# Rounded w_down factors made among the factors of q and k, weight loads two blocks ahead of rounding, and weight sums in other places

## The chip, the cores and the metric

One core of one Trainium2 chip runs the whole program. The metric is the device time of one execution in microseconds; the time before is the median of three runs, 1922.76 us (1920.47 to 1925.07). The core has five engines that run their own instruction streams in order and wait for one another by semaphores: PE multiplies matrices, ACT and DVE and POOL work elementwise, and SP issues most of the transfers (POOL issues the rest). Sixteen DMA engines move the data for all of them.

## The reference, cut to what matters

The kernel computes one layer of an encoder over 512 tokens of width 2048: a mixing part (attention of 8 heads beside a pooling part of 4 groups) and a feed-forward part (FFN) with a gate and a causal convolution.

```
h = rms_norm(x, pre_mix_g)
z = h @ w_in                      # q | k | v of 8 heads, and u
a = chunked_attention(q, k, v, rel_bias)
p = multiscale_pool(u, pool_w, pool_scale)
x = x + rms_norm(concatenate([a, p]) @ w_o, post_mix_g)
h = rms_norm(x, pre_ffn_g)
up = causal_dwconv(h @ w_up, conv_w, conv_b)
y = (gelu(up[:F]) * up[F:]) @ w_down
x = x + rms_norm(y, post_ffn_g)
```

Everything is float32. F is 5632.

## The kernel before

**Precision.** A float32 matrix goes to PE as two rounded parts: `split` (L138, L139) rounds it to a high part on ACT, and subtracts that from the source on DVE for the low part. `mm3` (L160, L162, L163) multiplies high by high, low by high and high by low. `mm2` (L168, L174) does a product that is 512 wide with the high part and 256 wide with the low one.

**Fast products.** q and k of heads 1 to 7, w_o and the FFN are multiplied in seven products of half-size blocks in place of eight. Some of the blocks are sums of weight blocks. For q and k they are made on DVE in the tiles where the weights were loaded. For w_o and w_down 1 MB sums are made in DRAM by transfers alone: `sums_in_dram` yields one copy, or one add onto a copy, at a time, and `more_sums(n)` takes the next n. There are 48 (32 for w_o, then 16 for w_down). While `paced` is set, they stand in POOL's queue behind a marker that waits for work that the program issued before; later, copies go through SP.

**Stages** and where they stand in the trace: q and k of head 0 (0 to 22 us); the first half of v (to 66, `v_steps(0)`); q and k of heads 1 to 7, the pairs (to 206); the second half of v beside the attention of heads 0 to 2 (to 282); u0 to u7 beside the other heads and the pooling (to 427); w_o (to some 590); then the FFN, whose first w_up products stand in a stage of their own (w10), and whose w_down products end the program.

**Weights.** Ordinary weights go through `Weights`: a list of blocks in the order of use, each a load of 512 KB on SP into a raw tile and a `split` into a hi and a lo tile of the ring `w4`; `prefetch` issues load and split together, three blocks ahead of PE.

**Pairs.** `Pairs` does the same for q and k. One pair k (one head) has seven products i; the products of neighbouring pairs are interleaved: (k+1,1), (k,6), (k+1,2), (k,7), (k+1,5), (k,4), (k+1,3). `load` (L467) loads four blocks per pair, named wx, ww, wz and wy; `make` splits the next factor (wfh, wfl) into the ring `w4`, which has four pairs of tiles, and then makes the next sum in place. `qk_product` and `qk_keep` multiply and take the products out of PSUM: products 1, 6, 7 and 4 of a pair share bank "a", which ACT empties (za, zm, zm, z) between them. At the end of a pair q and k go to DRAM (zqk, L596); the attention reads them back by head (zq, L673), multiplies by the norm's factor on DVE (L678) and splits them (qkh, qkl).

**Ready factors.** Three blocks of w_down, in six parts of 512 KB (`ready_parts`), are needed twice in rounded form. Each part (rw) is loaded, split, and its hi and lo halves are stored to DRAM (`ready_w`) during the u stage. Before, this is one more entry in the list of `Weights`: it stands behind the blocks of u0 to u5, in tiles of the ring `raw`, and `keep_ready` stores the halves (L284).

**Order.** PE's order is written out by hand in the program text. The other engines' orders, SP's queue among them, come from a scheduler that takes the instructions of the text as they become possible.

Of the kernel before, what the change touches and what calls it, by code (L numbers as in the profile page):

```python
# [15 lines left out]
P = 128  # L16
# [29 lines left out]
def f32(ap):  # L46
    return ap.bitcast(F32)
# [7 lines left out]
class Weights:  # L55


    def __init__(self, specs, load, ahead):
        self.specs, self.load, self.ahead, self.tiles, self.used = specs, load, ahead, [], 0
        self.limit = len(specs)  # L60

    def prefetch(self, n=None):
        self.prefetch_to(self.used + (self.ahead if n is None else n))
# [1 line left out]
    def prefetch_to(self, upto):  # L65
        upto = min(self.limit, upto)
        while len(self.tiles) < upto:
            self.tiles.append(self.load(*self.specs[len(self.tiles)]))

    def get(self, name, ahead=None):  # L70
        assert self.specs[self.used][0] == name, (self.specs[self.used][0], name)
# [8 lines left out]
def encoder_layer(ctx: ExitStack, tc: tile.TileContext, x, xT, vecs, rel, post_mix, post_ffn,  # L80
# [65 lines left out]
    def load_w(name, src, a, b):  # L146
        n = a * b
        raw = raw4(name + "r")
        if name[:2] == "rw":
            hi, lo = (big.tile([P, 1024], F32R, tag="raw", bufs=5, name=name + p) for p in "hl")  # L150
        else:
            hi, lo = w4(name + "h"), w4(name + "l")
        flat_ = len(src.shape) == 2
        load_w.last = nc.sync.dma_start(
            raw[:, :n] if flat_ else raw[:, :n].rearrange("p (a b) -> p a b", a=a), src).ins
        split(hi[:, :n], lo[:, :n], raw[:, :n])
        return tuple(v[:, :n].rearrange("p (a b) -> p a b", a=a) for v in (hi, lo))

# [102 lines left out]
    READY_AT = {0: (), 1: ()}  # L261
    ready_parts = [(at, j) for at in READY for j in range(2)]
    READY_OF = {0: (), 1: ready_parts}
    READY_U = {j: j for j in range(6)}

    def ready_spec(at, j):
        cc, i = at
        return (f"rw{cc}{i}_{j}", first_block(cc, i - 1, 0)[:, 2 * j:2 * j + 2, :], 2, 512)

    def v_and_ready_specs(g):  # L270
        specs = []
        for n, spec in enumerate(v_specs(g)):
            specs.append(spec)
            if n in READY_AT[g]:
                specs.append(ready_spec(*READY_OF[g][READY_AT[g].index(n)]))
        return specs

    def keep_ready(g, n):
        at = READY_U if g else {m: k for k, m in enumerate(READY_AT[0])}
        if n not in at:  # L280
            return
        (cc, i), j = READY_OF[g][at[n]]
        for dest, v in zip(ready_w[cc, i], weights.get(f"rw{cc}{i}_{j}")):
            nc.sync.dma_start(dest[:, 2 * j:2 * j + 2, :], f32(v))  # L284

    specs = v_and_ready_specs(0)
    FIRST_PART = len(specs)
    specs += v_and_ready_specs(1)
    for g in range(4):
        specs += u_specs(2 * g)  # L290
        if g:
            specs += pm_spec(g - 1)
        if 2 * g in READY_U:
            specs.append(ready_spec(*READY_OF[1][READY_U[2 * g]]))
        specs += u_specs(2 * g + 1)
        if 2 * g + 1 in READY_U:
            specs.append(ready_spec(*READY_OF[1][READY_U[2 * g + 1]]))
    for i in WO:
        for cc in range(2):
            specs += wo_specs(i, cc)  # L300
# [4 lines left out]
            specs += [(f"w{p}{u}_{i}", w_up[u, p, :, i // 2, :, i % 2 * 512:(i % 2 + 1) * 512].rearrange(  # L305
                "m p c -> p m c"), 2, 512) for i in range(4)]

    weights = Weights(specs, load_w, 3)
    weights.limit = FIRST_PART


# [38 lines left out]
                yield  # L350

    sums_step = sums_in_dram()


    RR = const.tile([P, 2, S], F32, name="RR")
# [41 lines left out]
    def v_steps(i, ps):  # L397
        for n, c in enumerate(VORDER[i]):
            w = weights.get(f"v{i}_{c}", 2 if (i, n) == (1, 0) else None)
            if not i:  # L400
                pairs.prefetch(3 - FIRST_PART + weights.used)
            for j in range(2):
                kb = 2 * c + j
                for t in range(NT):
                    mm3(ps[t], g_tokens(hT, kb, t), part(w, j), n == j == 0, n == 7 and j == 1)
                if j and not i:
                    keep_ready(i, n)
                    pairs.prefetch(3 - FIRST_PART + weights.used)
                yield

# [41 lines left out]
    class Pairs:  # L452
# [3 lines left out]
        def __init__(self):  # L456
            n = self.n = HEADS - 1
            place_of = {1: 0, 2: 2, 5: 4, 3: 6, 6: 8, 7: 10, 4: 12}
            begin = [(0, 1), (0, 2), (0, 5), (1, 1), (0, 3)]
            order = [(k, i) for _, k, i in sorted((7 * k + at, k, i) for k in range(n) for i, at in place_of.items())]  # L460
            self.order = begin + [at for at in order if at not in begin]
            self.order.insert(-2, (None, 0))
            self.raw, self.made, self.loaded, self.used = {}, [], 0, 0

        def load(self, k, i):
            def raw(what, tile_, m, kh):
                load_w.last = nc.sync.dma_start(tile_, w_qk[k + 1, m, kh]).ins  # L467
                self.raw[k, what] = tile_

            if i == 1:  # L470
                raw("x", raw4("wx") if not k else p0.tile([P, 1024], F32, tag="wx", bufs=3, name="wx"), 0, 0)
                raw("w", raw4("ww"), 1, 0)
            elif i == 2:
                raw("z", raw4("wz"), 0, 1)
            elif i == 5:
                raw("y", raw4("wy") if k else p0.tile([P, 1024], F32, tag="wx", bufs=3, name="wy"), 1, 1)

        def make(self, k, i):
            if k is None:
                weights.prefetch_to(FIRST_PART + 1)  # L480
                self.made.append(None)
                return
            x, w, y, z = (self.raw.get((k, what)) for what in "xwyz")
            hi, lo = w4("wfh"), w4("wfl")
            split(hi, lo, {3: y, 7: y, 2: z}.get(i, x))
            if i == 1:
                nc.vector.tensor_add(x, x, w)
            elif i == 5:
                nc.vector.tensor_add(x, x, y)
            elif i == 6:  # L490
                nc.vector.tensor_add(x, x, z)
            elif i == 3:
                nc.vector.tensor_add(y, y, w)
            self.made.append(tuple(v.rearrange("p (a b) -> p a b", a=8) for v in (hi, lo)))
# [11 lines left out]
                weights.prefetch_to(FIRST_PART + 1 + over)  # L506

        def get(self):
            self.used += 1
# [30 lines left out]
    def more_sums(n):  # L540
        for _ in range(n):
            next(sums_step, None)

    more_sums.paced = True

    BANK = {1: "a", 6: "a", 7: "a", 4: "a", 5: "g", 3: "g", 2: "d"}
    FIRST = 1, 5, 2
# [58 lines left out]
    for k, i in [at for at in pairs.order if at[0] is not None]:  # L606
        if k == pairs.n - 1 and i in (7, 4):
            if not steps:
                psv = [bank(f"v1_{t}") for t in range(NT)]
                steps = v_steps(1, psv)  # L610
                pairs.used += 1
# [19 lines left out]
    with tc.tile_pool(name="p1", bufs=2, reuse_waits="tile") as p1:  # L631
# [188 lines left out]
        for j in range(8):  # L820
# [62 lines left out]
    with tc.tile_pool(name="p2", bufs=1, reuse_waits="tile") as p2:  # L883
# [156 lines left out]
        for q in range(5):  # L1040
# [6 lines left out]
            if q:  # L1047
                gate_part(q - 1, 2)
                weights.prefetch(q)
        keep_x(2, turn_back.last)  # L1050
        for q in range(4):
# [696 lines left out]
```

## Time and profile before

| | before |
|---|---|
| median of 3 runs | 1922.76 us |
| lowest, highest | 1920.47, 1925.07 us |
| the profiled execution's own time | 1923.98 us |
| its span | 1922.2 us |
| its mean granted clock | 0.987 |
| PE busy | 1873.5 us, 97% |
| DVE, ACT, POOL busy | 80%, 56%, 16% |
| moved by DMA | 426.01 MB, 222 GB/s |

The durations below come from the profiled execution, whose span is the time from its first to its last instruction. A row of waits names the waiting instruction, the one that released it, and the total, the number and the longest of the waits in us. In a row of the chain of waits stand start, length and what ran; a DMA in it is the time from issue to landing. In a row of DMA issues stand the count, the size of one, and the median from issue to landing. q1 is SP's queue, q0 POOL's.

### The profile page before, as it was taken

What the parts mean: (1) busy time and instruction counts of PE and PEld (TensorE: products, weight loads), DVE (VectorE), ACT (ScalarE), POOL (GpSimd) and SP (SyncE); (2) the same over time, 40 slices, a digit from 0 to 9 for tenths busy, and PEclk for the clock granted to TensorE, in tenths of its full rate; (3) what the DMA queues carried; (4) which work ended last, traced back from release to release, by engine and by line L of the source; (5) the groups of instructions that cost most, each with busy time, mean ns of one, the idle gap of its engine ahead of it and who ended that gap; (6) DMA issues with size and microseconds to landing.
All of it is one profiled execution on the core that took longest, in us unless ns stands there. A gap on an engine that the chain in (4) does not pass through costs nothing.

```text
span 1922.2 us, 25415 instructions
## 1 busy us (share of the span) xinstructions
PE 1873.5 (97%) x9598; PEld 1593.1 (83%) x9598; DVE 1540.0 (80%) x1800; ACT 1082.9 (56%) x1376; POOL 301.5 (16%) x398
## 2 busy tenths in 40 slices
PE   9999989798999999999999999999999999999998
PEld 7888777676888888888888888888888888888886
DVE  6987667656778888888787888888887799898875
ACT  8655445334646566656566656656565665565553
POOL 3211110110000022222212121222211001101101
PEclk9999989898999999999999999999999999999999
DMA  7389988899787488888888888898988977876785
GB/s 257 123 264 287 328 204 307 216 309 273 263 250 283 140 212 202 200 196 199 208 200 200 204 199 205 200 199 195 208 188 273 349 228 176 197 197 171 172 237 143
DMA packets 139770, 426.01 MB, mean 222 GB/s; under 512 B 11968, under 2 KB 15424, under 8 KB 133952
## 3 DMA queue, kind: packets, MB, share of 16 engines
q0 software_dynamic: 54864, 173.56, 44.9%
q1 hardware_dynamic: 84784, 250.84, 37.4%
q8 instruction: 75, 1.23, 0.2%
q14 instruction: 47, 0.39, 0.1%
HBM read 370.35 MB, written 104.33 MB: 247 GB/s over the span
## 4 chain that ended last, share of the span: by engine, by line
PE 88%; DMA 6%; DVE 3%; ACT 2%; issue 1%; SPq 0%; DVEq 0%; POOL 0%; POOLq 0%; ACTq 0%
PE qa L168 18%; PE qa L174 10%; PE qg L168 9%; PE qg L174 5%; PE qd L168 5%; PE pa L160 4%; PE pa L162 4%; PE pa L163 4%; PE qd L174 2%; DMA rw_0r<-in_w_down 2%; PE m L163 2%; PE m L162 2%; PE m L160 2%; PE pg L160 2%; PE pg L162 2%; PE pg L163 2%
## 5 line engine op out<-in xcount | busy, mean ns | idle before, releaser
L138 ACT ACTIVATE wfh<-wx 128x1024 fp32r<-128x1024 f32 x192 | 203.5, 1060 | 153.8 <-PE qg L168 58.8
L168 PE MATMUL qa<-gT,wfh 128*128 128x512 f32 x1152 | 289.1, 393 | 0.0
L139 DVE TENSOR_TENSOR wfl<-wx,wfh 128x1024 fp32r<-128x1024 f32 x192 | 234.8, 1223 | 61.2 <-ACT wfh L138 45.5
L168 PEld LDWEIGHTS qa<-gT,wfh 128*128 128x128 f32 x1152 | 207.0, 188 | 37.5
L1365 POOL DMA_DIRECT2D wx<-in_w_up x122 | 104.6, 857 | 506.2 <-DVE wfl L139 478.0
L138 ACT ACTIVATE wfh<-wy 128x1024 fp32r<-128x1024 f32 x96 | 101.9, 1061 | 118.7 <-PE qg L168 62.0
L168 PE MATMUL qg<-h,wfh 128*128 128x512 f32 x656 | 165.7, 394 | 0.0
L174 PE MATMUL qa<-gT,wfl 128*128 128x256 f32 x1152 | 160.6, 282 | 0.0
L174 PEld LDWEIGHTS qa<-gT,wfl 128*128 128x128 f32 x1152 | 151.0, 190 | 4.4
L168 PEld LDWEIGHTS qg<-h,wfh 128*128 128x128 f32 x656 | 122.9, 188 | 28.0
L139 DVE TENSOR_TENSOR bl<-b,bh 128x2048 fp32r<-128x2048 f32 x56 | 127.4, 2288 | 22.5 <-ACT bh L138 11.7
L138 ACT ACTIVATE bh<-b 128x2048 fp32r<-128x2048 f32 x56 | 105.8, 1912 | 48.5 <-DVE b L1123 20.5
L139 DVE TENSOR_TENSOR wfl<-wy,wfh 128x1024 fp32r<-128x1024 f32 x96 | 117.2, 1221 | 14.2 <-ACT wfh L138 7.8
L160 PE MATMUL pa<-bh,ah 128*128 128x512 f32 x320 | 126.1, 394 | 0.0
L162 PE MATMUL pa<-bl,ah 128*128 128x512 f32 x320 | 125.8, 393 | 0.0
L163 PE MATMUL pa<-bh,al 128*128 128x512 f32 x320 | 125.5, 392 | 0.0
L139 DVE TENSOR_TENSOR wfl<-wz,wfh 128x1024 fp32r<-128x1024 f32 x48 | 58.8, 1224 | 55.2 <-PE qa L168 55.2
L168 PE MATMUL qd<-gT,wfh 128*128 128x512 f32 x384 | 95.7, 391 | 0.0
L174 PEld LDWEIGHTS qg<-h,wfl 128*128 128x128 f32 x656 | 89.4, 188 | 7.5
L174 PE MATMUL qg<-h,wfl 128*128 128x256 f32 x656 | 91.6, 282 | 0.0
L168 PEld LDWEIGHTS qd<-gT,wfh 128*128 128x128 f32 x384 | 72.0, 188 | 16.2
L168 PE MATMUL qa<-h,wfh 128*128 128x512 f32 x328 | 83.2, 395 | 0.0
(552 smaller groups left out, 4390.0 us busy)
## 6 DMA issues: line engine op xcount, KB each, us to landing
wx<-in_w_up POOLq DMA_DIRECT2D x122, 512.0 KB, 5.9
b<-in_w_down SPq DMA_DIRECT2D x32, 1024.0 KB, 6.8
wt<-in_w_o POOLq DMA_DIRECT2D x24, 1024.0 KB, 12.6
wx<-in_w_up SPq DMA_DIRECT2D x43, 512.0 KB, 5.5
wz<-in_w_up SPq DMA_DIRECT2D x41, 512.0 KB, 5.6
wy<-in_w_up SPq DMA_DIRECT2D x41, 512.0 KB, 4.6
wy<-in_w_up POOLq DMA_DIRECT2D x41, 512.0 KB, 6.2
sum<-part POOLq DMA_DIRECT2D x38, 512.0 KB, 6.1
```

What stands on the lines that cost most here:

```text
L138: rounded = nc.scalar.activation(hi, src, AF.Copy)
L139: rest = nc.vector.tensor_sub(lo, src, f32(hi))
L160: nc.tensor.matmul(ps, l[0], r[0], start=first, stop=False, skip_group_check=onto)
L162: nc.tensor.matmul(low, l[0], r[1], start=False, stop=False, skip_group_check=onto)
L163: nc.tensor.matmul(ps, l[1], r[0], start=False, stop=last, skip_group_check=onto)
L168: nc.tensor.matmul(ps, w[0][:, kb], pairs[kb][0], start=fresh and not kb, stop=last, skip_group_check=not fresh)
L174: nc.tensor.matmul(ps[:, sl], w[1][:, kb], pair[:, sl], start=False, stop=last, skip_group_check=not fresh)
L1365: nc.gpsimd.dma_start(self.raw[k, what], self.block(k, m, kh), accum_op=ALU.add)
```

## The change

`Weights` is now given a loader and a maker: a block is loaded `raws` = 2 blocks before it is split. `ready_spec`, `v_and_ready_specs` and `keep_ready` are gone; the six rw parts are entries (None, m) in the list of `Pairs`, each behind (m, 7). Their raw tile is one of its own (tag rw), hi and lo are a pair of `w4`, and the two stores are issued at the start of the next `make`. The sums are taken elsewhere: four more in the V stage (n = 4, 7, 10, 13), one fewer in the first head, six fewer in the u stage, one more in w_o's block 6, and two in w10. Their order and number stay.

```diff
@@ class Weights
+            while len(self.loaded) < min(self.limit, len(self.tiles) + 1 + self.raws):
+                self.loaded.append(self.load(*self.specs[len(self.loaded)]))
+            self.tiles.append(self.made(*self.loaded[len(self.tiles)]))
-            self.tiles.append(self.load(*self.specs[len(self.tiles)]))
@@ load_w, round_w
         raw = raw4(name + "r")
-        if name[:2] == "rw":
-            hi, lo = (big.tile([P, 1024], F32R, tag="raw", bufs=5, name=name + p) for p in "hl")
-        else:
-            hi, lo = w4(name + "h"), w4(name + "l")
...
+        return name, raw, n, a
+
+    def round_w(name, raw, n, a):
+        hi, lo = w4(name + "h"), w4(name + "l")
         split(hi[:, :n], lo[:, :n], raw[:, :n])
@@ the list of weights
-        if 2 * g in READY_U:
-            specs.append(ready_spec(*READY_OF[1][READY_U[2 * g]]))
...
-    weights = Weights(specs, load_w, 3)
+    weights = Weights(specs, load_w, round_w, 3, 2)
@@ class Pairs
-            self.order.insert(-2, (None, 0))
+            self.order.insert(-2, (None, None))
+            for m in range(len(ready_parts)):
+                self.order.insert(self.order.index((m, 7)) + 1, (None, m))
...
+            if k is None:
+                if i is not None:
+                    (cc, n), j = ready_parts[i]
+                    v = self.raw[k, i] = p0.tile([P, 1024], F32, tag="rw", bufs=1, name="rw")
+                    nc.sync.dma_start(v.rearrange("p (a b) -> p a b", a=2),
+                                      first_block(cc, n - 1, 0)[:, 2 * j:2 * j + 2, :])
...
         def make(self, k, i):
+            for dest, v in self.stores:
+                nc.sync.dma_start(dest, f32(v).rearrange("p (a b) -> p a b", a=2))
+            self.stores = []
             if k is None:
-                weights.prefetch_to(FIRST_PART + 1)
+                if i is None:
+                    weights.prefetch_to(FIRST_PART + 1)
+                else:
+                    (cc, n), j = ready_parts[i]
+                    pair = w4("rwh"), w4("rwl")
+                    split(*pair, self.raw.pop((k, i)))
+                    self.stores = [(dest[:, 2 * j:2 * j + 2, :], v) for dest, v in zip(ready_w[cc, n], pair)]
@@ the V stage
+        if n in (4, 7, 10, 13):
+            more_sums(1)
@@ the first heads
-            more_sums(1)
+            if h:
+                more_sums(1)
@@ the u stage
-            if j in READY_U:
-                keep_ready(1, j)
             if j < 7:
                 pool_keep(j // 2, j % 2, ps)
-                more_sums(1 + j % 2)
+                more_sums(1 if j % 2 or not j else 0)
@@ wo_product
-                more_sums(2 if i == 3 else 1)
+                more_sums(2 if i in (3, 6) else 1)
@@ w10
+        more_sums.paced = True
         for q in range(4):
             w = weights.get(f"w10_{q}")
+            if q in (0, 2):
+                more_sums(1)
```

The order of PE's instructions is the same in both kernels. Three places show how the others move. First ACT in the pairs, over one period of seven products; wfh is the high half of a factor of q and k, za, zb, zm and z are the evictions. Before:

```order
L587 ACTIVATE zm<-qa_1194 128x512
L138 ACTIVATE wfh<-wx 128x1024
L579 ACTIVATE zb<-qg_1478 128x512
L138 ACTIVATE wfh<-wz 128x1024
L594 ACTIVATE z<-qa_1194 128x256
L138 ACTIVATE wfh<-wy 128x1024
L138 ACTIVATE wfh<-wx 128x1024
L573 ACTIVATE za<-qa_1560 128x512
L138 ACTIVATE wfh<-wx 128x1024
L583 ACTIVATE zm<-qa_1377 128x512
```

and now:

```order
L140 ACTIVATE wfh<-wy 128x1024
L140 ACTIVATE rwh<-rw 128x1024
L568 ACTIVATE za<-qa_1609 128x512
L140 ACTIVATE wfh<-wx 128x1024
L578 ACTIVATE zm<-qa_1418 128x512
L140 ACTIVATE wfh<-wx 128x1024
L140 ACTIVATE wfh<-wy 128x1024
L140 ACTIVATE wfh<-wx 128x1024
L582 ACTIVATE zm<-qa_1418 128x512
```

rwh, the high half of a w_down part, stands once in each period. The second wfh<-wx behind it (the row after L578) is written into the tiles that rwh and its low half had; the zm of L582, which empties bank "a" of product 7, is three rows on.

Second, SP's queue from the end of the pairs to the first heads. Before:

```order
L596 DMA zqk_348<-z 128x1024
L673 DMA zq<-zqk_342 128x1024
L669 DMA bias<-in_rel 128x512
L154 DMA v_2r<-in_w_v 128x1024
L154 DMA v_3r<-in_w_v 128x1024
L154 DMA u_0r<-in_w_u 128x1024
L154 DMA u_1r<-in_w_u 128x1024
L596 DMA zqk_349<-z 128x1024
L673 DMA zq<-zqk_343 128x1024
L687 DMA vl_2099<-vd_350 128x2048
L154 DMA rw_0r<-in_w_down 128x2x512
```

and now:

```order
L591 DMA zqk_352<-z 128x1024
L152 DMA v_2r<-in_w_v 128x1024
L152 DMA v_3r<-in_w_v 128x1024
L152 DMA u_0r<-in_w_u 128x1024
L152 DMA u_1r<-in_w_u 128x1024
L591 DMA zqk_353<-z 128x1024
L667 DMA zq<-zqk_346 128x1024
L663 DMA bias<-in_rel 128x512
L681 DMA vl_2167<-vd_354 128x2048
L152 DMA u_0r<-in_w_u 128x1024
L667 DMA zq<-zqk_347 128x1024
```

The first zq (q and k of head 0) and its bias stood ahead of two v loads, two u loads and the store of the last head (zqk); now they stand behind these. rw is gone, and a further u load stands where the second head's zq was.

Third, SP's queue in the pairs, over one period, now:

```order
L449 DMA ww<-in_w_qk 128x1024
L591 DMA zqk_348<-z 128x1024
L449 DMA wz<-in_w_qk 128x1024
L468 DMA rw11h<-rwh 128x1024
L468 DMA rw11l<-rwl 128x1024
L456 DMA rw<-in_w_down 128x2x512
L449 DMA wx<-in_w_qk 128x1024
L449 DMA wy<-in_w_qk 128x1024
```

Before, a period was ww, zqk, wz, wx and wy; the two stores of rw and the load of the next part stand between wz and wx.

More of the change, by code (lines that the diff above doesn't have):

```diff
@@ L55, with __init__ @@
 class Weights:
-    def __init__(self, specs, load, ahead):
-        self.specs, self.load, self.ahead, self.tiles, self.used = specs, load, ahead, [], 0
-        self.limit = len(specs)
+    def __init__(self, specs, load, made, ahead, raws):
+        self.specs, self.load, self.made, self.ahead, self.tiles, self.used = specs, load, made, ahead, [], 0
+        self.limit, self.raws, self.loaded = len(specs), raws, []
     def prefetch(self, n=None):
@@ L259, in encoder_layer @@
     ready_w = {at: [dram.tile([P, CU, S], F32, name=f"rw{at[0]}{at[1]}{p}") for p in "hl"] for at in READY}
-    READY_AT = {0: (), 1: ()}
     ready_parts = [(at, j) for at in READY for j in range(2)]
[L263 to L286, printed above, removed]
+    specs = v_specs(0)
     FIRST_PART = len(specs)
-    specs += v_and_ready_specs(1)
+    specs += v_specs(1)
     for g in range(4):
@@ L292, in encoder_layer @@
             specs += pm_spec(g - 1)
-        if 2 * g in READY_U:
-            specs.append(ready_spec(*READY_OF[1][READY_U[2 * g]]))
         specs += u_specs(2 * g + 1)
-        if 2 * g + 1 in READY_U:
-            specs.append(ready_spec(*READY_OF[1][READY_U[2 * g + 1]]))
     for i in WO:
@@ L352, in encoder_layer, with more_sums @@
     sums_step = sums_in_dram()
+    def more_sums(n):
+        for _ in range(n):
+            next(sums_step, None)
+    more_sums.paced = True
     RR = const.tile([P, 2, S], F32, name="RR")
@@ L406, in v_steps @@
                 if j and not i:
-                    keep_ready(i, n)
                     pairs.prefetch(3 - FIRST_PART + weights.used)
@@ L461, in __init__ @@
             self.order = begin + [at for at in order if at not in begin]
-            self.order.insert(-2, (None, 0))
-            self.raw, self.made, self.loaded, self.used = {}, [], 0, 0
+            self.order.insert(-2, (None, None))
+            for m in range(len(ready_parts)):
+                self.order.insert(self.order.index((m, 7)) + 1, (None, m))
+            self.raw, self.made, self.loaded, self.used, self.stores = {}, [], 0, 0, []
         def load(self, k, i):
@@ L468, in raw @@
                 self.raw[k, what] = tile_
-            if i == 1:
+            if k is None:
[4 more added lines that the diff above has]
+                                      first_block(cc, n - 1, 0)[:, 2 * j:2 * j + 2, :])
+            elif i == 1:
                 raw("x", raw4("wx") if not k else p0.tile([P, 1024], F32, tag="wx", bufs=3, name="wx"), 0, 0)
@@ L508, in get @@
         def get(self):
+            while self.order[self.used][0] is None:
+                self.used += 1
             self.used += 1
@@ L538, in spread1 @@
         nc.vector.tensor_scalar_mul(RR[:, 1, :], R, -1.0)
[L540 to L544, printed above, removed]
     BANK = {1: "a", 6: "a", 7: "a", 4: "a", 5: "g", 3: "g", 2: "d"}
@@ L610, in encoder_layer @@
                 steps = v_steps(1, psv)
-                pairs.used += 1
             next(steps)
@@ L1050, in encoder_layer @@
         keep_x(2, turn_back.last)
+        more_sums.paced = True
         for q in range(4):
             w = weights.get(f"w10_{q}")
+            if q in (0, 2):
+                more_sums(1)
             for kb in range(4 * q, 4 * q + 4):
```

## The prediction

> **What bounds the kernel now.** I read first the busy table of the page, then the waits of TensorE by releaser, then windows cut at the stages.
>
> ```profile
> PE 1873.5 (97%) x9598; PEld 1593.1 (83%) x9598; DVE 1540.0 (80%) x1800; ACT 1082.9 (56%) x1376; POOL 301.5 (16%) x398
> ...
> PE pt L728 <- DVE s L717: 20.8, 7, 10.4
> PE m L160 <- ACT wo_3h L138: 7.6, 1, 7.6
> PE u L160 <- DVE ptl L139: 2.3, 1, 2.3
> ...
> 66.00:206.00 140.00, 140.00 (x795) 122.36 (x794) 117.75 (x141) 73.19 (x89) 19.53 (x63) 1.00 0.82 244
> 206.00:225.00 19.00, 19.00 (x93) 15.98 (x92) 14.13 (x26) 9.75 (x16) 1.31 (x4) 1.00 1.07 308
> 225.00:262.00 37.00, 26.65 (x123) 22.50 (x122) 20.88 (x49) 13.51 (x28) 3.90 (x8) 0.86 0.81 268
> 318.00:384.00 66.00, 51.11 (x224) 42.11 (x223) 45.83 (x109) 29.83 (x60) 8.19 (x16) 0.85 0.87 254
> 396.00:484.00 88.00, 76.70 (x320) 60.96 (x319) 57.36 (x90) 39.12 (x51) 10.01 (x16) 0.92 1.00 280
> ```
>
> PE is 97% busy and its instructions come in the same order after the change, so the time can move only by PE's idle time and its granted clock. A windows row reads: window, length, busy time of PE, PEld, DVE, ACT, POOL, then clock, DMA share, GB/s. Idle time is length minus PE; clock loss is PE times one minus the clock. The first attention heads (225:262) lose 10.4 + 26.65 x 0.14 = 3.7 us; the u stage (318:384) 14.9 + 7.7 = 22.6; the start of the w_o products (396:484) 11.3 + 6.1 = 17.4. That is 54 us, and 36.5 of the 48.7 us that PE idles in the whole span. The pairs stage (66:206), where q and k of heads 1 to 7 are made, loses nothing.
>
> What ends the three losses is in the ACT timeline and the chain of waits:
>
> ```profile
> 243.84 1.06 ACT L138 ACTIVATE rw_0h<-rw_0r 128x1024 fp32r<-128x1024 f32 x1 [12.07 <-DMA rw_0r<-in_w_down]
> 244.80 0.70 ACT L714 ACTIVATE s<-s,nm 128x512 f32<-128x512 f32 x1
> ...
> 225.06 18.70 DMA rw_0r<-in_w_down
> 246.37 1.75 PE pt L728 x7
> 265.26 0.98 PE pt L728 x7
> 329.60 17.15 DMA rw_0r<-in_w_down
> 379.18 7.47 DMA u_0r<-in_w_u
> 417.51 10.99 DMA pooled<-mx
> 444.24 14.47 DMA wo_3r<-in_w_o
> ```
>
> ACT takes its work in order. The rounding of a w_down factor (rw) stands ahead of a softmax exponential (s L714) and sits there until its load lands: 12.1 us at 243.8. PE then waits for the exponential to transpose it, and the seven transposes take 1.75 us where they take 0.98 later. At 346.8 it happens again behind a load of 17.2 us. At the w_o start no rw is in the way: a spill (pooled) takes 11 us, the ones behind it follow, and a weight lands 14.5 us late because the queues are full of weight sums.
>
> **The change, part by part.**
>
> *Removing rw from heads and u stage.* Six loads, roundings (1.06 ACT, 1.22 DVE) and twelve stores go, the three raw, hi and lo tiles leave the ring that the u loads use, and the u loads are issued one or two blocks earlier, so the 7.5 us u_0r load of the chain is no longer at its end. Seven sums fewer run beside it. Of 22.6 us I leave 4.6 (the ptl wait of 2.3 us is not touched, nor is a bit of clock): **-18**, bounds -22.6 and -8 (only the two rw waits, at half).
>
> *The start of w_o.* Its order doesn't change; only six sums fewer are issued in the u stage, with one more at w_o's seventh block. In 400:460 the sums land so:
>
> ```profile
> t<-in_w_down POOLq DMA_DIRECT2D x8, 1024.0 KB, 18.4
> pooled<-mx SPq DMA_DIRECT2D x2, 256.0 KB, 12.7
> ```
>
> With the backlog gone, spill, its read-back and the weight behind it each have to land in some 10 us or less for the wait to vanish; where fewer sums ran SP's loads did so (u_0r 7.5 at 379). Of 17.4 I leave 3: **-14**, bounds -17.4 and -5.
>
> *Heads, first wait.* rw's wait of 10.4 goes, but another comes. SP now issues q and k of head 0 (zq) behind two v loads, two u loads and the last store of the pairs (zqk); before, it stood ahead of all of these.
>
> ```profile
> 203.38 0.56 SPq L673 DMA_DIRECT2D zq<-zqk  x1
> 219.82 0.33 SPq L596 DMA_DIRECT2D zqk<-z  x1
> ...
> zq<-zqk SPq DMA_DIRECT2D x2, 512.0 KB, 10.0
> ...
> L678 DVE TENSOR_TENSOR zq<-zq,RR x8: 1216/1220/1225, 219.7 to 372.0; 128x1024 f32<-128x1024 f32 x8
> ...
> 225.41 0.28 PE L160 MATMUL s<-qkh 128*128 128x256 f32 x1
> ```
>
> So zq is issued at 219.8 + 0.4 instead of 203.4, lands 8 to 13 us later (10.0 is the median of two in 215:262) and takes 1.22 + 1.06 + 1.22 to be ready: 231.7 to 236.7. PE reaches the scores at 225.4 and waits 6 to 11 us. Against 10.4 + 3.7 that is **-1**, bounds -5 and +4 (a landing of 16 us).
>
> *The pairs stage.* Each of six periods (seven products of 2.8 us: 1.88 wide, 0.96 narrow) gets a load, two stores, 1.06 us of ACT and 1.22 of DVE. As work that fits: DVE goes from 117.75 to 125 of 140 us. What doesn't fit at once is a wait. hi and lo of rw take one of four slot pairs of the ring w4, and the second pair made after it, product 4's, is written into the same tiles, once the two stores have landed. On ACT that rounding (wfh) stands ahead of two more and of the eviction zm of product 7, and PE adds product 4 onto the bank that zm empties.
>
> ```profile
> 200.68 1.88 PE qg L168 x8
> 202.55 0.96 PE qg L174 x8
> ...
> L138 ACT ACTIVATE wfh<-wx 128x1024 fp32r<-128x1024 f32 x27 | 28.6, 1061 | 29.3 <-PE qg L168 9.4 <-PE qa L168 8.6 <-PE qa L174 7.5
> L583 ACT ACTIVATE zm<-qa 128x512 f32<-128x512 f32 x6 | 3.6, 600 | 4.8 <-PE qa L168 4.8
> ```
>
> From the moment the slot is free for rw: 1.4 us to the store's issue, its landing L, three roundings and zm (3 x 1.06 + 0.6 = 3.8). PE needs it after the narrow half and four products, 0.95 + 4 x 2.84 = 12.3. So a stall is L - 7.1. How long does such a store take? The nearest rows are the stores of z and the loads of the same size in the same stage (100:132, then 132:206):
>
> ```profile
> zqk<-z SPq DMA_DIRECT2D x2, 512.0 KB, 5.9
> wz<-in_w_qk SPq DMA_DIRECT2D x2, 512.0 KB, 8.5
> ...
> zqk<-z SPq DMA_DIRECT2D x4, 512.0 KB, 9.7
> wz<-in_w_qk SPq DMA_DIRECT2D x2, 512.0 KB, 8.7
> ```
>
> zqk and wz stand just ahead of the rw stores on SP, so the hi store ends one transfer after wz, at about 10 us; lower bound 2.6 (an rw store in the u stage with an empty queue), upper bound 16 (one behind two u loads):
>
> ```profile
> rw11h<-rw_1h SPq DMA_DIRECT2D x1, 512.0 KB, 2.6
> rw11l<-rw_1l SPq DMA_DIRECT2D x1, 512.0 KB, 15.9
> ...
> 101.11 0.98 POOL L326 DMA_DIRECT2D wt<-in_w_o  x1
> ...
> PE pt L728 <- DVE s L717: 9.3, 4, 3.0
> ```
>
> I take 10, as the copies and adds of the sums run in five of the six events (the first sum of the stage is issued at 101 us, a period after the first rw pair): 5 x 2.9 = 14.5 us idle. In the three stages above each idle microsecond brought another 0.48 of slow clock (17.5 on 36.5), so **+21**; bounds 0 and 5 x 8.9 x 1.48 = 66. The lo store lands some 2.7 us behind and holds DVE's lo half; that is needed one wide half later, so it sets nothing at this L. I keep to the middle, by the wz rows, since the load on SP's queue rises from five to eight half-megabyte transfers per 19.7 us and the sums are as many as before. By the Trainium skill's page "TensorE: Matmul & The Clock Gate" (Part 1, What's actually happening) the clock falls only after an idle window of about 3.4 us; by that rule stalls of 2.9 us would cost no clock and this term would be 14.5 and the sum 1905. The trace is against it: PE's longest wait in 318:384 is 3.0 us (the row above, the largest of that window), and the clock there is 0.85.
>
> *Weight sums.* Four copies move to the V stage ahead of the pairs, where DMA has room (48 to 96 us is the second of the page's 40 slices, at 123 GB/s), so each later sum runs four places earlier:
>
> ```profile
> GB/s 257 123 264 287 328 204 307 216 309 273 263 250 283 140 212 202 200 196 199 208 200 200 204 199 205 200 199 195 208 188 273 349 228 176 197 197 171 172 237 143
> ```
>
> Two adds go to the w10 products, ahead of POOL's first w_up loads; POOL is 16% busy over the span and the FFN's loads stand some blocks ahead of their use. 0, bounds 0 and +5, should one of these loads come late.
>
> *Loads two blocks ahead.* Past u this changes only when a load is issued; the raw tiles hold one more block. 0.
>
> **Sum:** -18 - 14 - 1 + 21 = -12 on the profiled execution's 1923.98 (span 1922.2 and 1.8 around it), 1912; the median of the runs lies 1.2 lower, so 1911.
>
> **Rivals.**
>
> A. *The stores land in time.* If the earlier sums leave the queue freer and L stays near 7, the pairs cost 0 to 4: -33 + 2 = -31, 1892. For it: zqk's 5.9 in 100:132. Against: DMA share is 0.82 already in 66:206.
>
> B. *The pairs stage fills the DMA queues* (the other side). From 85 to 206 SP moves
>
> ```profile
> q1 hardware_dynamic: 5374, 16.78, 38.8%
> ```
>
> 16.78 MB in 38.8% of 121 us, 2.8 us per MB. Its 9.4 MB more (six times three transfers of 0.52 MB) are 26 us in 140, which takes the share from 0.82 to 1.0. The stores then queue behind late loads, L is 13 for five events: 5 x 5.9 x 1.48 = 44, so +11, 1934. It decides from L = 11.5 (5 x 4.4 x 1.48 = 33, all of the gain). For it: the window 206:225 with a share of 1.07, out of which zq and zqk take 10 us and more. Against: PE lost nothing in that window (19.00 of 19.00). The Trainium skill's page "DMA: Bandwidth & Descriptors" (Queues, rings and completion order) says that a DMA engine goes round-robin between the queue rows it has work for; so SP would keep about half of the engines while a sum runs, which is what lets SP's queue fill.
>
> C. *The waits only move.* The exponentials are free of rw, but the u loads or vl and the spills set the end of the same stretches, as the pooled spill's 11.0 us do now; half of the 32 us gain stays away: -17 + 21 = +4, about 1926; with a milder pairs stage 1921, no change. For it: PE's waits on the pooled chain aren't touched by moving rw.
>
> **How the numbers follow.** The forecast 0.46 (own range 1898 to 1920), A 0.18, B 0.24, C 0.12. 0.2% is 3.8 us and about what a measurement of this kernel can tell from no change, so faster means below 1918.9: 0.41 of the forecast, A, and 0.01 of C give 0.60. Within 0.2%: 0.05 of the forecast, 0.03 of B, 0.06 of C, 0.14. Slower: 0.21 of B and 0.05 of C, 0.26. The range takes in A's value and B's: 1889 to 1936.
>
> **What would show it.** Right: in 66:206 PE waits of 2 to 4 us on ACT's zm, in five periods of 19.7 us, with wfh waiting on an rw store just before; the rw store lands in about 10 us; the wait for s L717 in 225:262 is replaced by one on qkh behind zq of 6 to 11 us; the window of the u stage at a clock above 0.95 with idle under 5 us; wo_3h's wait below 3 us. Wrong: no wait on zm in the pairs (then A), waits on zm of over 5 us or wfh waiting for w_qk loads (B), waits of 5 us or more left in the u stage or at wo_3h (C). PE idle time in the FFN stages, none now, would show a cost of the two late adds that I put at nothing.

## The result, and the profile after

The changed kernel takes 1920.49 us (median of 20 runs, 1916.99 to 1924.98), the kernel before 1921.81 us beside it. The ratio is 0.9995 with a 95% interval of 0.9988 to 1.0001: no difference that can be told. Forecast was a gain of 12 us.

The waits of TensorE by releaser, in the profile after (waiting instruction, releaser, total, number, longest):

```profile
PE qa L176 <- ACT zm L582: 21.4, 6, 5.8
PE s L162 <- ACT qkh L140: 11.0, 2, 9.8
PE s L164 <- DVE qkl L141: 1.6, 2, 0.9
PE pt L722 <- DVE pace L295: 1.1, 1, 1.1
PE idle L133 <- DVE mhalf L129: 1.1, 1, 1.1
PE m L164 <- DVE wo_3l L141: 1.0, 1, 1.0
```

None of the waits of before is left: 20.8 us for s, 7.6 for wo_3h, 2.3 for ptl. In their place stand six waits in the pairs stage on the eviction zm, and one on qkh of head 0. The windows, cut at the stages of this run, which lie later (the columns are those of the prediction):

```profile
66.00:240.00 174.00, 152.53 (x796) 131.54 (x795) 124.31 (x150) 76.90 (x96) 19.11 (x37) 0.92 0.89 267
240.00:256.00 16.00, 16.00 (x79) 13.52 (x78) 10.10 (x18) 7.55 (x14) 3.76 (x33) 1.00 0.71 242
256.00:290.00 34.00, 23.57 (x105) 19.56 (x104) 19.38 (x44) 11.69 (x22) 3.43 (x10) 0.85 1.00 257
290.00:350.00 60.00, 60.00 (x302) 51.17 (x301) 43.89 (x105) 29.72 (x61) 3.29 (x9) 1.00 0.72 218
350.00:405.00 55.00, 51.73 (x255) 43.58 (x254) 44.88 (x107) 28.67 (x60) 5.55 (x10) 0.97 0.82 226
405.00:500.00 95.00, 94.04 (x426) 77.91 (x425) 74.08 (x107) 53.36 (x68) 6.81 (x9) 1.00 0.91 265
```

The account by stage in us, idle time plus clock loss, worked out as in the prediction:

| stage | lost before | forecast change | lost after | change |
|---|---|---|---|---|
| pairs | 0 | +21 | 21.5 + 12.2 = 33.7 | +33.7 |
| first heads | 14.1 | -1 | 10.4 + 3.5 = 13.9 | -0.2 |
| u stage | 22.6 | -18 | 3.3 + 1.6 = 4.9 | -17.7 |
| start of w_o | 17.4 | -14 | 1.0 + 0 = 1.0 | -16.4 |
| sum | 54.1 | -12 | 53.5 | -0.6 |

Three terms came out within 2.5 us. The pairs stage took 12.7 us more than its term, and with that the whole gain. The two profiled spans differ by 2.4 us (1922.2 and 1919.8); 1.8 of them lie outside these four stages or in the rounding of the clock.

The ACT timeline shows one of the six waits, and the rows of the rw tile show all of them (engine, line, what waited, us and times; last the time from issue to landing of its six stores):

```profile
150.97 1.06 ACT L140 ACTIVATE wfh<-wx 128x1024 fp32r<-128x1024 f32 x1 [10.11 <-DMA rw11h<-rwh]
151.94 1.04 ACT L140 ACTIVATE wfh<-wy 128x1024 fp32r<-128x1024 f32 x1
152.88 1.04 ACT L140 ACTIVATE wfh<-wx 128x1024 fp32r<-128x1024 f32 x1
153.83 0.57 ACT L582 ACTIVATE zm<-qa 128x512 f32<-128x512 f32 x1
...
ACT wfh L140: 47.3, 6
...
DMA to landing us min/median/max: 5.8/10.2/13.1
```

That is the chain of the prediction: a rounding waits 10.1 us for the store rw11h to land, two more roundings and zm stand behind it. The six events, with the store's landing L from the DMA issues of each stretch and PE's wait on zm from the waits of that stretch:

| store | L | L - 7.1 | PE's wait |
|---|---|---|---|
| 1 (issued at 93.9) | 5.8 | none | 4.1 |
| 2 | 9.4 | 2.3 | 1.9 |
| 3 | 13.1 | 6.0 | 5.8 |
| 4 | 11.5 | 4.4 | 4.0 |
| 5 | 10.7 | 3.6 | 3.2 |
| 6 | 9.8 | 2.7 | 2.4 |

The mean L is 10.05 us, the 10 that was taken. Behind the first store the formula fails for another reason, seen on SP's timeline and the tile's rows:

```profile
90.11 0.33 SPq L449 DMA_DIRECT2D ww<-in_w_qk  x1
93.51 0.33 SPq L449 DMA_DIRECT2D wx<-in_w_qk  x1
93.93 0.38 SPq L468 DMA_DIRECT2D rw01h<-rwh  x1
...
L140 ACT ACTIVATE rwh<-rw x6: 1058/1060/1062, 87.1 to 215.1; 128x1024 fp32r<-128x1024 f32 x6
```

rwh was ready at 88.2, but its store stood on SP behind the loads ww and wx, which wait for their tiles: each is issued just after an instruction on DVE that ends at 90.1 and at 93.5. The store was issued 5.7 us after rwh was ready. The prediction has 1.4 us to the issue; here it was 6.8 from the start of rwh, 5.4 more, and 5.8 + 5.4 - 7.1 is the 4.1 us that PE waited.

The clock after the waits, from windows of the same run that begin when PE resumes:

```profile
103.63:108.00 4.37, 4.37 (x16) 3.87 (x17) 4.37 (x7) 2.02 (x3) 1.45 (x2) 0.61 0.58 156
127.07:131.00 3.93, 3.93 (x14) 3.45 (x15) 3.93 (x6) 1.05 (x2) 1.33 (x2) 0.57 1.10 263
154.46:159.00 4.54, 4.54 (x16) 4.03 (x17) 4.54 (x7) 1.89 (x3) 0.78 (x2) 0.58 0.84 278
180.12:185.00 4.88, 4.88 (x16) 4.20 (x17) 4.88 (x7) 2.22 (x3) 1.35 (x2) 0.50 0.86 206
205.74:210.00 4.26, 4.26 (x16) 3.69 (x17) 4.26 (x6) 1.61 (x3) 0.67 (x2) 0.60 1.09 215
229.61:234.00 4.39, 4.38 (x16) 3.81 (x17) 4.39 (x6) 1.74 (x3) 0.61 (x2) 0.61 0.89 268
```

A wait of 1.9 us (before 127.07) and one of 5.8 us (before 154.46) are followed by the same stretch at about 0.6 of the clock. The six windows lose 11.2 of the 12.2 us of slow clock in the stage.

### The profile page after: what moved, and what is told of

Read it like the earlier page. It is cut to its first block, busy times and chain, and to the rows that moved or that the text cites. A ratio compares the mean times of both kernels' runs of the same rounds, so it can differ in the third digit from the quotient of the medians.

```text
span 1919.8 us, 25463 instructions
## 1 busy us (share of the span) xinstructions
PE 1873.3 (98%) x9598; PEld 1595.0 (83%) x9598; DVE 1539.6 (80%) x1799; ACT 1080.7 (56%) x1376; POOL 299.0 (16%) x394
## 4 chain that ended last, share of the span: by engine, by line
PE 90%; DMA 5%; DVE 2%; ACT 2%; issue 1%; SPq 0%; DVEq 0%; ACTq 0%; POOLq 0%
PE qa L170 17%; PE qa L176 9%; PE qg L170 9%; PE qg L176 4%; PE qd L170 4%; PE pa L162 4%; PE pa L164 4%; PE pa L165 4%; PE m L164 3%; PE m L165 3%; PE m L162 2%; PE qd L176 2%; PE pg L162 2%; PE pg L164 2%; PE pg L165 2%; PE v L162 1%
## 5 line engine op out<-in xcount | busy, mean ns | idle before, releaser
L170 PE MATMUL qa<-gT,wfh 128*128 128x512 f32 x1152 | 295.7, 399 | 0.0
L170 PEld LDWEIGHTS qa<-gT,wfh 128*128 128x128 f32 x1152 | 212.1, 193 | 39.1
L176 PE MATMUL qa<-gT,wfl 128*128 128x256 f32 x1152 | 165.7, 288 | 21.8 <-ACT zm L582 21.4
L141 DVE TENSOR_TENSOR wfl<-wy,wfh 128x1024 fp32r<-128x1024 f32 x96 | 117.2, 1221 | 12.2 <-ACT wfh L140 4.0
L141 DVE TENSOR_TENSOR wfl<-wz,wfh 128x1024 fp32r<-128x1024 f32 x48 | 58.8, 1224 | 55.4 <-PE qa L170 53.5
## 6 DMA issues: line engine op xcount, KB each, us to landing
wt<-in_w_o POOLq DMA_DIRECT2D x24, 1024.0 KB, 14.8
```

Of the source, the lines that this page charges most:

```text
L141: rest = nc.vector.tensor_sub(lo, src, f32(hi))
L170: nc.tensor.matmul(ps, w[0][:, kb], pairs[kb][0], start=fresh and not kb, stop=last, skip_group_check=not fresh)
L176: nc.tensor.matmul(ps[:, sl], w[1][:, kb], pair[:, sl], start=False, stop=last, skip_group_check=not fresh)
```

## The experiments

Each time is a median of 4 to 10 runs, beside runs of the kernel before on the same chip (1919.9 to 1921.8 us).

**1. One z tile: why head 0's zq is late.** In the order of instructions SP issues zq behind four loads and a store. Loads two blocks ahead could be the cause, or memory: the pairs' pool has 4 KB more for the raw rw tile, and the pool of the attention is laid out after it.

```diff
-        return p0.tile([P, 2, S], F32, tag="z", bufs=2, name="z")
+        return p0.tile([P, 2, S], F32, tag="z", bufs=1, name="z")
```

> The change, with one z tile instead of two in the pool of the pairs, so that this pool is as large as it was before the rw tile came into it. Theory: the 10.4 us that PE waits for qkh and qkl of head 0 come from the pool's 4 KB more: the tiles of the attention then lie over the last evictions of the pairs, and SP may load zq only behind the last store. With the pool at its old size zq stands ahead of the v and u loads again, the wait falls from 10.5 to under 2 us, with some 3 us of slow clock: 1920 - 11 to 13, so 1907 to 1910. Rival 1, zq was late because loads are issued two blocks earlier: nothing changes, 1920. Rival 2, the single z tile makes each head's store hold back the next one: waits on z in the pairs, 1920 or slower.

1914.67 us, ratio 0.9971 (0.9962 to 0.9981). zq stands ahead of v_2r again and the wait on qkh for head 0 is gone; on qkh 1.2 us are left, at another head. (The profiled execution was the slowest of the ten, 1919.24 us.)

```profile
PE qa L176 <- ACT zm L582: 17.6, 5, 4.8
PE qg L170 <- ACT zb L574: 7.0, 2, 5.9
...
PE s L162 <- ACT qkh L140: 1.2, 1, 1.2
```

Of the 7.0 us on zb, 5.9 are new: ACT waits at 80 us to spill the second half of v into the one z tile until the first half's store has landed. So the theory holds for the wait on zq, and rival 2 for this one place, which takes back about half of the gain.

**2. rw's raw tile in the ring: the same without that wait.**

```diff
-                    v = self.raw[k, i] = p0.tile([P, 1024], F32, tag="rw", bufs=1, name="rw")
+                    v = self.raw[k, i] = raw4("rw")
```

> The change, with rw's raw tile taken from the ring of raw tiles instead of the pool of the pairs, whose size is then that of the kernel before; both z tiles stay. Theory: the wait of 10.5 us for qkh and qkl of head 0 goes as in the run with one z tile, without that run's 5.9 us stall behind the spill of v (ACT waited there for the store of the only z tile): 1920 - 11 to 14, so 1906 to 1909. Rival: the ring of raw tiles is short by one, the loads of q's and k's weights come late, and the pairs stage gives back 5 us or more: 1912 or more.

1909.38 us, ratio 0.9937 (0.9918 to 0.9956), just above what was expected: 11 us for the wait on head 0. Both ways of giving the pool its old size took it away. That the tiles of the attention lie over those of the pairs is the reason given for it; the runs show the size and the order, not the addresses. The pairs keep their waits (18.8 us on zm).

**3. Holding rw's tiles longer.** A 128x1 read on DVE, placed behind the N-th factor made after rw, keeps rw's two places from being given away; loads, roundings and stores stay. In the change the hi place is used again two factors later; with N = 2, 3 and 4 three, four and five later. Of the edit, with N = 2:

```diff
+                    self.held = [2, pair]
...
             self.made.append(tuple(v.rearrange("p (a b) -> p a b", a=8) for v in (hi, lo)))
+            if self.held:
+                self.held[0] -= 1
+                if not self.held[0]:
+                    for v in self.held[1]:
+                        with tc.issue_after(split.rest):
+                            nc.vector.tensor_copy(early[:, :1], f32(v)[:, :1])
+                    self.held = []
```

> The change, with a tiny DVE read of rw's hi and lo tiles placed behind the second factor made after them, so that the tiles are given to a much later factor and no rounding of q's and k's factors waits for rw's stores. Loads, roundings and stores are as many as in the change. Theory: the stores' landing is what stops ACT; the six waits on zm (21.4 us) go, and with them some 11 us of slow clock in 90 to 240 us: 1920 - 25 to 33, so 1888 to 1895. Rival (the DMA queues are full, from the prediction's case B): the stage stays as long, PE then waits on wfh behind late loads of q's and k's weights, and no more than 8 us come back: 1912 or more.

1913.45 us, ratio 0.9964 (0.9952 to 0.9977): less than expected. The time lies in the rival's range, but PE does not wait behind loads of q's and k's weights, as the rival has it: six waits on zm remain, at 14.8 us instead of 21.4. One factor more was not enough; at four of the six ACT now waits for the lo store, whose place a later hi half has taken:

```profile
151.12 1.06 ACT L140 ACTIVATE wfh<-wx 128x1024 fp32r<-128x1024 f32 x1 [5.15 <-DMA rw11l<-rwl]
```

> Both: rw's tiles read once more behind the third factor made after them (their place is then used four factors later), and one z tile. Theory: the two waits are apart in time and add: 1920 - 12 - 29, so 1876 to 1885. Rival: with both gone the sums and the u loads are reached earlier and the w_o wait comes back (as in the kernel before, 7.6 us and more): 1890 or more.

1899.75 us, ratio 0.9892 (0.9877 to 0.9906). This is slower than the theory and again in the rival's range, but the w_o wait that the rival named is not back (1.6 us on wo_3l). No wait on zm is left; 11.0 us are on zb, 5.9 of them the wait of experiment 1 on the one z tile, and 4.2 on wfl. No run holds the tiles for three factors with both z tiles, so what each part gives by itself isn't shown.

> As the run that holds rw's tiles for three factors with one z tile, with the second half of v's spill put into the tile of zm, so that ACT does not wait there for the store of the first half. rw's raw tile is its own, so its load is early. Theory: of that run's waits the 5.9 us at 85 us goes, those of 1 to 4 us on zb and wfl stay (stores of 12 us and more): 1900 - 6 to 9, so 1891 to 1894. Rival: with the early wait gone the sums and stores come closer together and the later waits grow by as much: 1897 or more.

There is one z tile here too, and the second half of v's spill goes into the tile of zm. 1894.40 us, ratio 0.9860 (0.9843 to 0.9876), at the upper end of what the theory had.

> As the run with rw's raw tile in the ring, with rw's hi and lo read once more behind the fourth factor made after them, so that their places are used five and six factors later (in the change two and three, in the run that held them for three it was four and five). Theory: each factor later gives a store 2.8 us more, so stores of up to about 15 us stop nothing; no waits on zm or zb over 1.5 us, 1878 to 1890. Rival: with the tiles held so long only three pairs are left for q's and k's factors, PE catches up with DVE, and waits on wfl appear (as one of 4.2 us did with three): 1892 to 1900.

1901.29 us, ratio 0.9889 (0.9865 to 0.9914): above the range of theory and rival. In the profiled execution, the fastest of the four (1894.88 us, the others 1900.78 to 1902.69), zm still costs 12.6 us, and not for the pairs of tiles that the rival named:

```profile
133.99 1.06 ACT L140 ACTIVATE rwh<-rw 128x1024 fp32r<-128x1024 f32 x1 [4.94 <-DMA rw<-in_w_down]
```

ACT waits for rw's own load, which comes late out of the ring of raw tiles.

> The same with rw's tiles held for four factors, their places used five and six factors later. Theory: rw's load is early here, unlike in the run with the ring's raw tile, and a store has up to 15 us, so the pairs stage waits under 5 us in all: 1880 to 1888, faster than both kernels. Rival: three pairs of tiles for q's and k's factors are too few over that long a stretch, PE waits on wfl or zm for 8 us or more in all: 1892 or more.

Again with one z tile and the spill in the tile of zm. 1892.44 us, ratio 0.9852 (0.9837 to 0.9866): faster than both kernels. The time lies in the rival's range, but its mechanism does not show: on zm are 2.0 us and on wfl none.

```profile
PE qg L170 <- ACT zb L582: 5.9, 3, 2.4
PE qa L176 <- ACT wfh L140: 2.7, 2, 2.5
PE qa L176 <- ACT zm L586: 2.0, 2, 1.4
```

From 21.4 us of waits in the pairs, 10.6 are left, in seven pieces. Hardly any of it is behind a store of rw (ACT waits for one once, 1.0 us). At the three on zb ACT waits for DVE, and DVE, two instructions earlier, for a store out of the one z tile:

```profile
189.26 0.60 ACT L582 ACTIVATE zb<-qg 128x512 f32<-128x512 f32 x1 [4.40 <-DVE zm L591]
187.00 0.42 DVE L595 TENSOR_TENSOR z<-za 128x256 f32<-128x256 f32 x1 [2.35 <-DMA zqk<-z]
```

DVE waits so before each of the three (2.5, 2.3 and 2.4 us). The zm of 1.4 and 0.7 us stand behind a rounding of rw that waits for its own load (2.6 and 2.0 us), and the wfh of 2.5 us behind the load of wy (DVE waits 4.9 us for it).

**4. The stores in ACT's queue.**

```diff
-                nc.sync.dma_start(dest, f32(v).rearrange("p (a b) -> p a b", a=2))
+                nc.scalar.dma_start(dest, f32(v).rearrange("p (a b) -> p a b", a=2))
```

> As the run with rw's raw tile in the ring, with rw's twelve stores issued by ACT into its own queue instead of SP's. The tiles are reused as early as in the change. Theory: a store takes 10 us because it stands in SP's queue behind wz and beside the sums; alone in its queue it lands in 4 to 7 us, ACT's wait for it and most of PE's six waits on zm (21.4 us in the change) go: 1875 to 1885. Rival 1, the DMA engines as a whole are full and it lands in 9 us or more: 1900 to 1908. Rival 2, ACT's issue waits hold up its in-order work.

1905.63 us, ratio 0.9918 (0.9899 to 0.9936). Against the 1909.38 of the same kernel with SP's queue little is gained, and the intervals overlap. The hi stores land in 3.5 to 9.7 us, median 8.9, against 4.0 to 10.6, median 8.7, there. So rival 1 fits: SP's order is not what makes the landing long. The waits changed all the same: ACT waits 6.1 us for hi stores instead of 34.4, but 28.1 instead of 20.2 for the loads of rw out of the ring, and PE's waits are now 17.0 us on the zm of product 6 (L578, four, up to 9.0) behind these. The DMA share in 85 to 240 us, stalls included, is 0.95 here and 0.94 in the change.

**5. The sums where they were.**

```diff
-        if n in (4, 7, 10, 13):
-            more_sums(1)
...
-                more_sums(1 if j % 2 or not j else 0)
+                more_sums(1 + j % 2)
...
-            if q in (0, 2):
-                more_sums(1)
```

> The change, with the weight sums in the places of the kernel before (none in the V stage, one in the first head's scores, ten in the u stage, none in w10). Theory: the six fewer sums in the u stage are what frees the w_o start: the wait for wo_3h is back at 5 to 8 us with slow clock behind it, and the u stage waits 3 to 6 us more, while the pairs stage changes little: 1928 to 1940. Rival: it is rw's removal that frees the u stage and the w_o start, and the places of the sums matter little: 1918 to 1923, with no wait on wo_3h above 2 us.

1934.13 us, ratio 1.0074 (1.0059 to 1.0089): the theory's time, and its wait on wo_3h. Without the sums' new places the change is 14 us slower than the kernel before.

```profile
PE qa L176 <- ACT zm L580: 17.5, 6, 4.4
PE s L162 <- ACT qkh L140: 11.7, 1, 11.7
PE m L162 <- ACT wo_3h L140: 6.7, 1, 6.7
PE u L162 <- DVE ptl L141: 3.5, 1, 3.5
...
350.00:405.00 55.00, 51.48 (x256) 43.59 (x255) 45.30 (x112) 28.97 (x59) 8.11 (x16) 0.97 0.92 255
405.00:500.00 95.00, 85.30 (x373) 69.24 (x372) 64.18 (x102) 44.67 (x59) 10.01 (x16) 0.96 0.96 272
```

The theory missed the u stage (350:405): it loses 3.5 + 1.5 us here, about as in the change (4.9), so there rw's leaving is enough with the sums in their old places. The w_o start loses 9.7 + 3.4 us; there it is not.

**6. No loads ahead** (raws = 0 in the call of `Weights`).

> The change with raws = 0: a block's load is issued with its rounding again, as in the kernel before; all else as in the change. Theory: once rw has left the list and the ring, the u loads have room enough, so little of the u stage's gain comes from loading ahead: 1918 to 1926, u stage waits up to 4 us more. Rival: the loads ahead are what keeps ACT from waiting in the u stage, and 8 us or more of its 18 us gain goes: 1928 or more.

1923.17 us, ratio 1.0011 (0.9999 to 1.0022): theory. The loads ahead are worth little (some 3 us), and the u stage does without them: it loses 2.9 + 1.6 us, in 350:405 as in the change (4.9). zq is late without them too, so they are not why.

**7. The sums alone.** The kernel before with the `more_sums` lines of the change, and nothing else.

> The kernel before with nothing but the new places of the weight sums; rw stays in the u stage, loads are issued with their rounding. Theory: the run with the old sums lost 14 us, 6.7 of them at wo_3h, so the places of the sums free the w_o start by themselves: the 7.6 us wait for wo_3h falls under 2 us and its slow clock with it, and the waits behind rw in the heads and the u stage (20.8 us) shrink by a quarter to a half: 1921 - 15 to 22, so 1899 to 1906, with nothing to pay in the pairs. Rival: rw's loads and stores keep the queue full up to w_o whatever the sums do: 1915 or more.

1895.18 us, ratio 0.9865 (0.9850 to 0.9880), better than the theory's best. The waits, and the windows of the first heads, of the u stage and of the w_o start:

```profile
PE pt L731 <- DVE s L720: 11.2, 5, 6.0
PE u L160 <- DVE ptl L139: 2.9, 1, 2.9
...
PE m L162 <- DVE wo_3l L139: 0.8, 1, 0.8
...
66.00:206.00 140.00, 140.00 (x795) 122.39 (x794) 119.57 (x144) 74.07 (x90) 20.30 (x67) 1.00 0.89 263
...
223.00:255.00 32.00, 25.97 (x114) 21.73 (x113) 19.59 (x41) 12.28 (x23) 3.31 (x6) 0.89 1.06 264
...
318.00:385.00 67.00, 57.73 (x264) 47.76 (x264) 50.15 (x119) 32.29 (x65) 5.57 (x10) 0.90 0.89 263
385.00:500.00 115.00, 114.21 (x512) 94.40 (x511) 91.09 (x120) 65.02 (x82) 7.97 (x10) 1.00 1.01 306
```

The w_o start loses 0.8 us instead of 17.4, the heads 6.0 + 2.9 instead of 14.1, the u stage 9.3 + 5.8 instead of 22.6, and the pairs nothing.

**8. The change without moving rw:** sums and loads ahead, rw in the u stage as before.

> The kernel before with the new places of the sums and with loads two blocks ahead of rounding; rw alone stays in the u stage, in the list of weights, so this is the change without the moving of rw. Theory: moving rw cost about what it saved and more, since the sums alone gave 26 us; the loads ahead bring rw and u earlier to ACT, so some of the remaining 16 us of waits in the heads and the u stage go: 1880 to 1892. Rival: raw, hi and lo tiles of rw share the ring of five with the loads ahead, which then wait for it, and nothing more is gained: 1893 to 1898.

1894.28 us, ratio 0.9865 (0.9849 to 0.9882): the rival; loads ahead add nothing to the sums. One row of its windows is enough for the pairs:

```profile
66.00:206.00 140.00, 140.00 (x794) 122.45 (x793) 119.20 (x144) 74.15 (x90) 20.26 (x67) 1.00 0.89 264
```

So of the change's three parts the sums give 26 us, the loads ahead about none, and moving rw takes 26 back (1920.5 against 1894.3). The parts do not simply add: with rw moved the sums' new places give only 14 us (1934.1 against 1920.5), since rw's leaving frees the u stage without them.

## Why the prediction was wrong

- *u stage, -18:* right in size (-17.7) and in its main source, rw leaving ACT's queue: with the sums in their old places the stage loses 5.1 us (experiment 5). The sums alone bring 22.6 to 15.1 (experiment 7).
- *Start of w_o, -14:* right in mechanism and nearly in size (-16.4). The sums alone do all of it (experiment 7), and without them the stage loses 13.1 us, 6.7 of them the wait on wo_3h (experiment 5).
- *Heads, -1:* right (-0.2), for the wait that was named: zq issued at 253.8, landed at 266.5, 12.7 us later. Why SP issues it so late the prediction did not ask. The pool of the pairs grew by the raw tile; at its old size the wait is gone, and 11 us with it (experiments 1 and 2).
- *Pairs, +21: the step that failed, by its size.* The mechanism, the threshold of 7.1 us and the landing of 10 us are as forecast; the table of the six events follows L - 7.1 within 0.4 us from the second on. Three sizes in the term were too small. First, the event without sums was counted as free; its store landed in 5.8 us, but was issued 5.4 us later than the formula has it, behind loads waiting on SP: 4.1 us. Second, the other five stores landed in 10.9 us on average, not 10, and a stall is the excess over a threshold, so 0.9 us more of landing made 17.3 us of waits out of 14.5 (the formula gives 19.0): 2.8 us. Third, slow clock was taken as 0.48 us for each idle microsecond; it was 12.2 on 21.5, 0.57. Of the 5.2 us that this is above the 7 of the forecast, 3.3 come with the longer waits at the old rate and 1.9 with the higher rate. 4.1 + 2.8 + 5.2 = 12.1 of the 12.7 us. That these waits are the price of moving rw is shown from both sides: the stage waits for nothing where rw stays (experiment 8), and holding rw's tiles for four factors takes away ACT's waits for rw's stores but for 1.0 us, from 47.3 (experiment 3).
- *Sums and loads ahead at nothing* in the later stages: w10 and the FFN show no wait above 0.3 us, so the two late adds cost nothing there.
- *Rivals:* B named the right stage, but its mechanism, an L of 13, fits one store of six. Its price for the stage, 44 us, is 10 above the measured 33.7, and the forecast's 21 is 13 below. C did not happen: no wait over 1.2 us is left in the u stage or at w_o. That its milder value, 1921, is the measured time is luck.
- *The clock:* three of the six waits, 1.9, 2.4 and 3.2 us long, were followed by some 4 us at 0.57 to 0.61 of the clock, like the longer ones. The Trainium skill's page "TensorE: Matmul & The Clock Gate" (Part 1, What's actually happening) has the clock fall after an idle window of about 3.4 us; here the measurement decides against it, as the prediction did.

What stays open: how fast the pairs would be with rw's tiles held for four factors and two z tiles, since 5.9 of the 10.6 us that still wait there come from the one z tile. And the fastest kernel here (1892.4 us, experiment 3 with four factors) has an interval that overlaps that of the sums alone (1895.2 us), so whether rw can be moved to the pairs at a gain isn't shown.

## What to carry to other kernels

Price each part of a change by itself, also against the others' absence: here one part gave 26 us, another took 26, and the sum said "no change"; and what the sums gave depended on where rw was. When an extra tile is pushed through a ring that in-order engines share, ask when its place is used again and how long its store takes to land there; every landing beyond that is a wait, once per turn. A larger pool can delay work of the next stage that has nothing to do with it.

## What the hardware showed unexpectedly

Waits of 2 us can cost as much clock as waits of 6. In the change PE ran 3.93 us at a clock of 0.57 after 1.9 us of waiting, and 4.54 us at 0.58 after 5.8: about 1.7 to 2.4 us lost for each of the six waits (PE times one minus the clock). But not every wait costs it. With rw's tiles held for four factors, in the same stage, the four waits of 0.7 to 1.8 us left the clock at 1.00, and the two of 2.4 and 2.5 us were followed by 4 us at 0.57 and 0.63. Two of these windows, after 1.8 and after 2.4 us:

```profile
143.40:147.40 4.00, 4.00 (x21) 3.46 (x22) 4.00 (x8) 1.17 (x2) 0.78 (x2) 1.00 1.03 408
189.91:193.91 4.00, 4.00 (x13) 3.23 (x14) 4.00 (x8) 1.17 (x2) 0.67 (x2) 0.57 1.08 284
```

The length of a wait does not decide it alone: with the tiles held for three factors and the spill in the tile of zm, one of 3.09 us left the clock at 1.00 and one of 3.05 brought it to 0.61. What decides it there is not shown.

And a queue of its own did not make a 512 KB store much faster (8.9 us median against 8.7) where the DMA share was 0.95. Taking sums out of a full stretch did make transfers faster: with the sums' places alone changed (experiment 7), the 1 MB sums into w_down's tiles landed in 12.0 us in 380:470 (six, on POOL's queue), against 18.4 before (eight), and the pooled spills beside them in 3.7 us against 10.4.

```profile
t<-in_w_down POOLq DMA_DIRECT2D x6, 1024.0 KB, 12.0
pooled<-mx SPq DMA_DIRECT2D x4, 256.0 KB, 3.7
```
